# Value weights multiplied into the output weights inside a fused mLSTM and attention layer

## The chip, the cores and the metric

The kernel runs on one core of one Trainium2 chip. The metric is the device time of one execution in microseconds, the median over several runs; lower is better. A profiled execution stands beside the runs: it gives, for each instruction, the engine, the start and the duration.

The engines are TensorE (PE; its weight loads are PEld), VectorE (DVE), ScalarE (ACT), GpSimd (POOL) and SyncE (SP), which issues most transfers.

## The reference

One layer of a bidirectional encoder for 2048 tokens of width 1024, all in float32:

```python
h = rms_norm(x, g_mix_norm)
z = h @ w_in                       # 1024 -> 2000, split into nine parts
y_a = mlstm_group(q_m, k_m, v_m, o_m, gates, ...)          # (S, 512)
# group B: latent attention, 4 heads
q  = (rms_norm(c_q, g_cq) @ w_uq).reshape(B, S, 4, 192)
kv = (rms_norm(c_kv, g_ckv) @ w_ukv).reshape(B, S, 4, 256)
k_nope, v = kv[..., :128], kv[..., 128:]
# k gets a shared rotary part; q and k are normalised per head, rotary is applied
p = softmax(q_h @ k_h.T * 192 ** -0.5)
y_b = concat over heads of p @ v_h                          # (S, 512)
x = x + concat(y_a, y_b) @ w_out
h = rms_norm(x, g_ffn_norm)
x = x + square(relu(h @ w_ff1)) @ w_ff2
```

A fact of this algebra that the change uses: with `cn` the normalised latent of 128 numbers per token and `Wv_h` the 128x128 value part of `w_ukv` for head `h` (rows scaled by `g_ckv`), `v_h = cn @ Wv_h`. So `(p_h @ v_h) @ w_out[512 + 128 h :]` equals `(p_h @ cn) @ (Wv_h @ w_out[512 + 128 h :])`.

## The kernel before

Matmuls run as three products of a high and a low part (`mm3`): `split` casts a float32 tile to the high part on ACT and subtracts it on DVE (or on POOL where `eng` says so) for the low part.

The program has these stages. **First phase** (`phase_a`): tokens are normalised and transposed into `hh` and `hl`, eight tiles of 128 tokens at a time (two halves); all columns of `w_in` are projected. In each half there are eight `rest` tiles and then three blocks of eight tiles: `z_v`, `z_qk` (with a convolution on DVE, results in `ot`) and `z_o` (output gate). Each tile or channel group is 24 matmuls into one of two `pz` banks. `load_w` loads and splits the weights of a block; the split weights lie in pool `a_w`, the raw ones in `a_raw`.

Between those tiles `tick` places the work of latent attention (MLA), tile by tile, in four parts. `mla_a1` normalises the latent (`cn`, one buffer), transposes and splits it (`cTh`, `cTl`). `mla_a2` multiplies it with `wukh`, `wukl` (from `w_ukv`, keys and values of four heads interleaved, 1024 columns) and with the query weights into four `pm` banks, and forms squares on ACT. `mla_b1` copies the values out (`vn`, stored to `d_va`) and forms keys and queries on DVE. `mla_b2` transposes these and stores them to `d_kn`, `d_qn`, `d_kr`, `d_qr`. In this phase a scheduler orders the instructions by priority (program order, with `urgent` ahead) and by when they are expected to be ready.

**Attention** (`attention`): written out by hand, one step `g` for each score tile of 128 queries by 512 keys: five matmuls (`score`), the maximum on DVE, the exponential on ACT (`softmax`), four transposes and a split (`transpose_group`), and one `pv` step (three matmuls with `vh`, `vl`). `load_q`, `load_k`, `load_v` bring raw tiles into eight buffers of pool `stage`; `split_q`, `split_k`, `split_v` split them. Per head there are four K tiles and four V tiles. Two calls of `next(work)` per pair of steps bring in the mLSTM: first `mlstm_prelude` (gate tables, mostly small DVE operations), then `mlstm_steps`. Its loads `mlstm_v` and `mlstm_k` go through SP's queue.

**Output projection** (`OutProj`): `weights` loads and splits `w_out`; `load_b2` loads its lower half once more, for sums of weights. **Feed-forward** (`FeedForward`): two layers, each as seven products of halves.

SP's queue issues in order: a transfer that waits holds up all that stand behind it. Pools of attention lie over the pools of the first phase: `stage`, `k_sb` and `q_sb` on the right side of the memory, where the constants of latent attention (`wukh`, `wukl`, `wuqh`, ...) and its working tiles lay; `p_sb` over `hh`.

Of the kernel before, what the change touches and what calls it, by code (L numbers as in the profile page):

```python
# [8 lines left out]
F32 = mybir.dt.float32  # L9
# [79 lines left out]
def scratch(c, ctx):  # L89
# [9 lines left out]
    c.d_kr = dr.tile([NH, ROPE, S], F32, name="d_kr")  # L99
    c.d_va = dr.tile([S, 512], F32, name="d_va")  # L100
    c.d_ya = dr.tile([S, 512], F32, name="d_ya")
# [17 lines left out]
def phase_a(c):  # L119
    nc, tc = c.nc, c.tc  # L120
    with ExitStack() as st:
# [4 lines left out]
        hp = pool("a_h", 2)  # L126
        wp = pool("a_w", 9)
        rp = pool("a_raw", 5)
# [129 lines left out]
        def load_wu():  # L258
            for k in range(2):
                for j in range(2):  # L260
                    raw = rp.tile([P, 512], F32, name="raw")
                    cs = slice(j * 384, (j + 1) * 384)
                    nc.sync.dma_start(raw[:, :384], c.w_uq[k * P:(k + 1) * P, cs])
                    split(nc, wuqh[k][:, cs], wuql[k][:, cs], raw[:, :384], gcq[:, k:k + 1])
            for j in range(2):
                raw = rp.tile([P, 512], F32, name="raw")
                cs = slice(j * 512, (j + 1) * 512)
                nc.sync.dma_start(raw, c.w_ukv[:, cs])
                split(nc, wukh[:, cs], wukl[:, cs], raw, gcq[:, 2:3])

# [38 lines left out]
        def mla_a1(t, zr):  # L309
# [18 lines left out]
            with urgent():  # L328
                split(nc, ch, cl, pt[:, 0:3, :])
            mla_env[t] = [zr, ms3, ch, cl]  # L330

        def mla_a2(t):

            zr, ms3, ch, cl = mla_env[t]
            pk, pq = [], []
            for j in range(2):
                o = psM.tile([P, 512], F32, name="pm")
                cs = slice(j * 512, (j + 1) * 512)
                mm3(nc, o, ch[:, 2, :], cl[:, 2, :], wukh[:, cs], wukl[:, cs], True, True)
                pk.append(o)  # L340
            for j in range(2):
# [8 lines left out]
            qs = [pq[h // 2][:, (h % 2) * DH:(h % 2 + 1) * DH] for h in range(NH)]  # L350
            ks = [pk[h // 2][:, (h % 2) * 256:(h % 2) * 256 + NOPE] for h in range(NH)]
            for h in range(NH):
# [7 lines left out]
            rsqrt(c, r8, ms8, 8)  # L360
            mla_env[t] = [zr, pk, qs, ks, r8]

        def mla_b1(t):

            tok = slice(t * P, (t + 1) * P)
            zr, pk, qs, ks, r8 = mla_env[t]
            vn = mp.tile([P, NH, DV], F32, name="vn")
            for j in range(2):
                nc.scalar.copy(vn[:, 2 * j:2 * j + 2, :],
                               pk[j].rearrange("p (h d) -> p h d", h=2)[:, :, NOPE:])  # L370
            nc.sync.dma_start(c.d_va[tok, :], vn.rearrange("p h d -> p (h d)"))
            kpe = mp.tile([P, 1, ROPE], F32, name="kpe")
# [160 lines left out]
        for half in range(2):  # L533
# [27 lines left out]
            if half == 0:  # L561
# [5 lines left out]
                nc.sync.dma_start(c.d_r, rrow)  # L567
            nxt = []
            for blk in range(3):
                w = load_w((CV, CQ, CO)[blk], 512)  # L570
                if half == 0 and blk == 1:
                    load_r()
                for i in range(8):
                    n = blk * 8 + i
                    tick(n + 6 * half)
                    if half == 0 and blk == 2 and i >= 4:
                        prep_t(8 + i - 4, nxt)
                        if i == 7:
# [160 lines left out]
def mlstm_steps(c, pool, ps, ld):  # L739
# [185 lines left out]
    for n, grp in enumerate(groups):  # L925
        outs = [outer(kws.pop(ch), ld.pop(ch)[0]) for ch in grp]
        yield
        for k, ch in enumerate(grp):
            new = back[ch - 1] = advance(1, NT - 1 - ch, outs[k])
            if ch > 4:  # L930
                nc.sync.dma_start(c.d_C[ch - 1], new)
                ld[ch - 4] = mlstm_v(c, ch - 4), mlstm_k(c, ch - 4)
            if k == 0 and n + 1 < len(groups):
# [69 lines left out]
def attention(c, keep, drain, project):  # L1003

    nc, tc = c.nc, c.tc
    with ExitStack() as st:
# [41 lines left out]

        def load_v(h, j):
            raw = vraw[h, j] = rp.tile([P, 512], F32, name="raw").rearrange("p (k d) -> p k d", k=4)  # L1050
            nc.sync.dma_start(raw, c.d_va[j * 512:(j + 1) * 512, h * DV:(h + 1) * DV].rearrange(
                "(k p) d -> p k d", p=P))

        def split_v(h, j):
            raw = vraw.pop((h, j))
# [3 lines left out]
            V[h, j] = vh, vl  # L1059

# [80 lines left out]
        def pv(b, j, k):  # L1141
            h = b // NB
# [39 lines left out]
        load_v(0, 0)  # L1182
        load_v(0, 1)
        work = mlstm()
        def next_v(bp, j):
            h = bp // NB + 1
            if bp % NB == NB - 1 and h < NH:
                split_v(h, j)
                if j < 2:
                    load_v(h, j + 2)  # L1190

        for g0 in range(0, 16 * N, 2):
# [4 lines left out]
            for g in pair:  # L1197
                bp, n = divmod(g - 22, 16)
                if bp >= 0:
                    pv(bp, *divmod(n, 4))  # L1200
                    if n % 4 == 3:
                        next_v(bp, n // 4)
            if g0 % 16 == 4 and g0 > 32:
                out(g0 // 16 - 2)()
            for g in pair:
# [27 lines left out]
                if h < NH - 1:  # L1233
# [107 lines left out]
class OutProj:  # L1341
# [19 lines left out]
    def weights(self):  # L1361
# [985 lines left out]
```

## Time and profile before

| | us |
|---|---|
| median of 3 runs | 2545.44 (2545.09 to 2545.82) |
| profiled execution, time | 2542.08 |
| its span, first to last instruction | 2540.3 |
| PE busy | 2523.7 (99%) |
| PEld busy | 2111.3 (83%) |
| DVE busy | 1726.1 (68%) |
| ACT busy | 1293.7 (51%) |
| POOL busy | 380.7 (15%) |

The granted TensorE clock was 1.000 over the span. The first phase ends near 458 us, attention near 1130 us, the output projection and the first feed-forward layer near 1925 us. In the rows of the profile, `pm<-wukh,cTh` reads "output tile <- inputs" (the moving operand first, then the stationary one for matmuls); an `x` count follows, and times in brackets are idle time of the engine ahead of the row, with what ended it.

### The profile page before, as it was taken

The page shows a single profiled execution, that of the slowest core. Times are in us where ns is not written, and L with a number is a line of the kernel's source. Part 1 is how long each engine was busy: PE and PEld are TensorE (multiplying, and loading weights), DVE is VectorE, ACT ScalarE, POOL GpSimd, SP SyncE. Part 2 cuts the span into 40 slices and gives each one's busy share as a digit, 9 for nine tenths or more (in the row PEclk, how much of TensorE's full clock was granted, in tenths as well). Part 3 has the DMA queues.
Part 4 walks back from the last instruction along what each step waited for, and adds up shares of the span by engine and source line. Part 5 has one row for each costly group of instructions (what it writes and reads, how often), then busy time and mean ns, then how long its engine had stood idle before and what let it go on. Part 6 is the DMA issues. An engine that isn't in the chain of part 4 may idle for free. (4 is left out here: it accounts for less than half of the span.)

```text
span 2540.3 us, 35812 instructions
## 1 busy us (share of the span) xinstructions
PE 2523.7 (99%) x12380; PEld 2111.3 (83%) x12380; DVE 1726.1 (68%) x3286; ACT 1293.7 (51%) x2900; POOL 380.7 (15%) x428
## 2 busy tenths in 40 slices
PE   9999999999999999999999999999999999999999
PEld 7888888788888888888888888888888888888887
DVE  5585467766667667678788777977775577665433
ACT  6454444656767677674455555655554323332332
POOL 1211111223323332200000000000000232322000
PEclk9999999999999999999999999999999999999999
DMA  5434234355344343235786555654448544444552
GB/s 177 143 112 152 91 113 137 111 146 134 89 115 114 85 121 102 63 110 193 235 271 227 196 189 185 244 166 149 142 153 300 201 149 142 145 145 145 211 183 95
DMA packets 295931, 392.53 MB, mean 155 GB/s; under 512 B 32262, under 2 KB 176965, under 8 KB 295749
## 3 DMA queue, kind: packets, MB, share of 16 engines
q1 hardware_dynamic: 293284, 385.78, 48.0%
q10 hardware_dynamic: 2464, 4.46, 0.5%
q8 instruction: 97, 1.59, 0.3%
q14 instruction: 86, 0.70, 0.1%
HBM read 258.51 MB, written 131.64 MB: 154 GB/s over the span
## 5 line engine op out<-in xcount | busy, mean ns | idle before, releaser
L69 PE MATMUL pd<-w2h,uh 128*128 128x512 f32 x896 | 348.8, 389 | 0.1
L70 PE MATMUL pd<-w2l,uh 128*128 128x512 f32 x896 | 348.7, 389 | 0.0
L71 PE MATMUL pd<-w2h,ul 128*128 128x512 f32 x896 | 348.7, 389 | 0.0
L54 DVE TENSOR_TENSOR ul<-ur,uh 128x1024 fp32r<-128x1024 f32 x110 | 149.3, 1357 | 251.8 <-ACT uh L53 251.8
L53 ACT CAST uh<-ur 128x1024 fp32r<-128x1024 f32 x110 | 115.7, 1052 | 396.0 <-PE pd L70 382.4
L54 DVE TENSOR_TENSOR ptl<-ptp,pth 128x512 fp32r<-128x512 f32 x248 | 171.1, 691 | 190.0 <-ACT pth L53 188.9
L53 ACT CAST pth<-ptp 128x512 fp32r<-128x512 f32 x248 | 143.4, 578 | 157.7 <-PE ptp L1137 157.1
L2015 DVE TENSOR_TENSOR e<-pu,e 128x512 f32<-128x512 f32 x224 | 151.3, 689 | 88.7 <-PE pu L71 87.7
L69 PEld LDWEIGHTS pd<-w2h,uh 128*128 128x128 f32 x896 | 168.2, 188 | 35.4 <-DVE e L2015 0.5
L71 PEld LDWEIGHTS pd<-w2h,ul 128*128 128x128 f32 x896 | 168.2, 188 | 34.9
L70 PEld LDWEIGHTS pd<-w2l,uh 128*128 128x128 f32 x896 | 168.2, 188 | 34.8
L1106 ACT ACTIVATE p<-p,nm 128x512 f32<-128x512 f32 x256 | 185.8, 726 | 2.6 <-DVE nm L1099 2.6
L1095 DVE TENSOR_SCALAR_CACHE_REDUCE p<-ps 128x512 f32<-128x512 f32 x256 | 167.4, 682 | 15.2 <-PE ps L1094 15.1
L2179 POOL TENSOR_TENSOR r<-wr,r 128x512 f32<-128x512 f32 x48 | 81.5, 1697 | 621.1 <-DMA wr<-in_w 590.0
L69 PE MATMUL pz<-wh,hh 128*128 128x512 f32 (+1 forms) x384 | 149.5, 391 | 1.7 <-ACT vo L495 0.7
L71 PE MATMUL pz<-wh,hl 128*128 128x512 f32 (+1 forms) x384 | 150.0, 391 | 0.0
L70 PE MATMUL pz<-wl,hh 128*128 128x512 f32 (+1 forms) x384 | 149.2, 389 | 0.1
L2018 ACT ACTIVATE e<-e 128x512 f32<-128x512 f32 x128 | 80.9, 632 | 120.5 <-DVE e L2015 114.0
L1137 PE MATMUL ptp<-ident,p 128*128 128x128 f32 x992 | 130.6, 274 | 0.5 <-DVE ptl L54 0.3
L1137 PEld LDWEIGHTS ptp<-ident,p 128*128 128x128 f32 x992 | 113.6, 140 | 14.1 <-issue 1.4
L1090 PE MATMUL ps<-kh,qh 128*128 128x512 f32 x256 | 112.8, 441 | 2.4 <-DVE p L1095 2.4
L1883 ACT CAST r<-w1raw 128x512 fp32r<-128x512 f32 x104 | 64.6, 622 | 92.5 <-PE pu L71 92.5
(526 smaller groups left out, 6463.5 us busy)
## 6 DMA issues: line engine op xcount, KB each, us to landing
d_u<-e SPq DMA_DIRECT2D x224, 256.0 KB
ur<-d_u SPq DMA_DIRECT2D x110, 512.0 KB
wr<-in_w SPq DMA_DIRECT2D x96, 256.0 KB
w1raw<-in_w SPq DMA_DIRECT2D x42, 512.0 KB
raw<-in_w_in SPq DMA_DIRECT2D x48, 256.0 KB
r<-in_w SPq DMA_DIRECT2D x22, 512.0 KB
mb<-d_M SPq DMA_DIRECT2D x32, 256.0 KB
acc<-d_x SPq DMA_DIRECT2D x16, 512.0 KB
```

Of the source, the lines that this page charges most:

```text
L53: r = nc.scalar.copy(hi, src)
L54: (eng or nc.vector).tensor_tensor(lo, src, hi.bitcast(F32), op=ALU.subtract)
L69: nc.tensor.matmul(out, ah, bh, start=first, stop=False, skip_group_check=more)
L70: nc.tensor.matmul(out, ah, bl, start=False, stop=False, skip_group_check=more)
L71: nc.tensor.matmul(out, al, bh, start=False, stop=last, skip_group_check=more)
L1090: nc.tensor.matmul(o, qh[:, qs], kh, start=True, stop=False)
L1095: nc.vector.tensor_scalar(p, o, SCALE, None, op0=ALU.mult, op1=ALU.max, accum_out=maxes[b, a][:, j:j + 1])
L1106: nc.scalar.activation(p, p, AF.Exp, bias=maxes[b, a], accum_out=dens[b][:, a, j:j + 1])
L1137: nc.tensor.transpose(pt[:, k, :], p[:, k * P:(k + 1) * P], c.ident)
L2015: nc.vector.tensor_tensor(out, o, t, op=ALU.add)
L2018: nc.scalar.activation(t, t, AF.Relu)
L2179: nc.gpsimd.tensor_tensor(R, wr, R, op=ALU.subtract)
```

## The change

The value half of `w_ukv` is no longer multiplied with every token. It is scaled, transposed, split, and multiplied with the lower half of `w_out` once (`value_rows`), 8 products of 128x512, stored to `d_wv` on ACT's queue. Attention's `pv` multiplies the probabilities with `cn` (stored to `d_cn`), the same for all heads, so that it is loaded and split once. Both places that loaded the lower half of `w_out` load `d_wv`. Some loads and splits in attention change place or engine.

```diff
-    c.d_va = dr.tile([S, 512], F32, name="d_va")
+    c.d_cn = dr.tile([S, P], F32, name="d_cn")
+    c.d_wv = dr.tile([NH * P, D], F32, name="d_wv")
...
-        wp = pool("a_w", 9)
+        wp = pool("a_w", 10)
...
-            for j in range(2):
-                raw = rp.tile([P, 512], F32, name="raw")
-                cs = slice(j * 512, (j + 1) * 512)
-                nc.sync.dma_start(raw, c.w_ukv[:, cs])
-                split(nc, wukh[:, cs], wukl[:, cs], raw, gcq[:, 2:3])
+            raw = load_ukv(0)
+            split(nc, wukh[:, 0:512], wukl[:, 0:512], raw, gcq[:, 2:3])
+
+        def load_ukv(i):
+            raw = rp.tile([P, 512], F32, name="raw")
+            nc.sync.dma_start(raw.rearrange("p (h d) -> p h d", h=NH),
+                              c.w_ukv.rearrange("p (h t d) -> p h t d", h=NH, t=2)[:, :, i, :])
+            return raw
+
+        def value_rows():
+            raw = load_ukv(1)
+            nc.scalar.activation(raw, raw, AF.Copy, scale=gcq[:, 2:3])
+            yield
+            pt = psT.tile([P, 4, P], F32, name="pt")
+            for h in range(NH):
+                nc.tensor.transpose(pt[:, h, :], raw[:, h * P:(h + 1) * P], c.ident)
+            split(nc, wukh[:, 512:], wukl[:, 512:], pt.rearrange("p h d -> p (h d)"))
+            yield
+            pieces = {}
+
+            def load(n):
+                h, j = divmod(n, 2)
+                pieces[n] = rp.tile([P, 512], F32, name="raw")
+                nc.sync.dma_start(pieces[n], c.w_out[512 + h * P:512 + (h + 1) * P, j * 512:(j + 1) * 512])
+
+            def part(n):
+                wh = wp.tile([P, 512], F32R, name="wh")
+                wl = wp.tile([P, 512], F32R, name="wl")
+                split(nc, wh, wl, pieces.pop(n))
+                if n + 3 < 2 * NH:
+                    load(n + 3)
+                parts.append((wh, wl))
+
+            parts = []
+            for n in range(3):
+                load(n)
+            part(0)
+            yield
+            for n in range(2 * NH):
+                h, j = divmod(n, 2)
+                if n + 1 < 2 * NH:
+                    part(n + 1)
+                wh, wl = parts.pop(0)
+                o = psM.tile([P, 512], F32, name="pm")
+                hs = slice(512 + h * P, 512 + (h + 1) * P)
+                mm3(nc, o, wukh[:, hs], wukl[:, hs], wh, wl, True, True)
+                w = ep.tile([P, 520], F32, name="ot")[:, 0:512]
+                nc.scalar.copy(w, o)
+                nc.scalar.dma_start(c.d_wv[h * P:(h + 1) * P, j * 512:(j + 1) * 512], w)
+                if n < 6:
+                    yield
...
         def mla_a2(t):
-            zr, ms3, ch, cl = mla_env[t]
-            pk, pq = [], []
-            for j in range(2):
-                o = psM.tile([P, 512], F32, name="pm")
-                cs = slice(j * 512, (j + 1) * 512)
-                mm3(nc, o, ch[:, 2, :], cl[:, 2, :], wukh[:, cs], wukl[:, cs], True, True)
-                pk.append(o)
+            zr, ms3, ch, cl, cn = mla_env[t]
+            nc.sync.dma_start(c.d_cn[t * P:(t + 1) * P, :], cn[:, 256:384])
+            pq = []
+            pk = psM.tile([P, 512], F32, name="pm")
+            mm3(nc, pk, ch[:, 2, :], cl[:, 2, :], wukh[:, 0:512], wukl[:, 0:512], True, True)
...
         def mla_b1(t):
-            vn = mp.tile([P, NH, DV], F32, name="vn")
-            for j in range(2):
-                nc.scalar.copy(vn[:, 2 * j:2 * j + 2, :],
-                               pk[j].rearrange("p (h d) -> p h d", h=2)[:, :, NOPE:])
-            nc.sync.dma_start(c.d_va[tok, :], vn.rearrange("p h d -> p (h d)"))
...
+            rows = value_rows()
             for blk in range(3):
...
                     tick(n + 6 * half)
+                    if half and n >= 14:
+                        next(rows, None)
...  # mlstm_steps
         outs = [outer(kws.pop(ch), ld.pop(ch)[0]) for ch in grp]
+        for ch in grp:
+            if ch > 4:
+                ld[ch - 4] = mlstm_v(c, ch - 4), mlstm_k(c, ch - 4)
         yield
...
                 nc.sync.dma_start(c.d_C[ch - 1], new)
-                ld[ch - 4] = mlstm_v(c, ch - 4), mlstm_k(c, ch - 4)
...  # attention
-        def load_v(h, j):
-            raw = vraw[h, j] = rp.tile(...)
-            nc.sync.dma_start(raw, c.d_va[j * 512:(j + 1) * 512, h * DV:(h + 1) * DV].rearrange(...))
+        def load_v(j):
+            raw = vraw[j] = rp.tile(...)
+            nc.sync.dma_start(raw, c.d_cn[j * 512:(j + 1) * 512, :].rearrange("(k p) d -> p k d", p=P))
...
-            vh, vl = V[h, j]
+            vh, vl = V[j]
...
-            ld = {ch: (mlstm_v(c, ch), mlstm_k(c, ch)) for ch in range(NT - 1, NT - 5, -1)}
-            yield from mlstm_prelude(c, psM)
+            for n, _ in enumerate(mlstm_prelude(c, psM)):
+                if n == 10:
+                    ld = {ch: (mlstm_v(c, ch), mlstm_k(c, ch)) for ch in range(NT - 1, NT - 5, -1)}
+                yield
...
-                    split_k(h + 1, u - 3, nc.vector if u == 6 else nc.gpsimd)
-                    if u == 6:
-                        load_v(h + 1, 0)
-                        load_v(h + 1, 1)
+                    split_k(h + 1, u - 3, nc.gpsimd if u == 4 else nc.vector)
...
-                if g in (6, 8, 10, 12):
-                    split_v(0, g // 2 - 3)
-                    if g < 10:
-                        load_v(0, g // 2 - 1)
+                if g in (2, 4, 6, 8):
+                    load_v(g // 2 - 1)
+                if g in (16, 18, 20, 22):
+                    split_v(g // 2 - 8)
...  # OutProj.weights and OutProj.load_b2
-            nc.sync.dma_start(raw, c.w_out[k * P:(k + 1) * P, :])
+            nc.sync.dma_start(raw, c.d_wv[(k - 4) * P:(k - 3) * P, :])
...
-                                     self.c.w_out[(4 + k) * P:(5 + k) * P, half * 512:(half + 1) * 512])
+                                     self.c.d_wv[k * P:(k + 1) * P, half * 512:(half + 1) * 512])
```

The value splits of the later heads (`next_v`, called behind `pv`) and the two first loads of values ahead of the loop go as well. In `value_rows`, the call at `n` = 14 loads the value half, 15 transposes it, 16 loads the first pieces, 17 to 22 form one product each, 23 the last two, each ahead of that step's projection tile.

More of the change, by code (lines that the diff above doesn't have):

```diff
@@ L329, in mla_a1 @@
                 split(nc, ch, cl, pt[:, 0:3, :])
-            mla_env[t] = [zr, ms3, ch, cl]
+            mla_env[t] = [zr, ms3, ch, cl, cn]
         def mla_a2(t):
-            zr, ms3, ch, cl = mla_env[t]
-            pk, pq = [], []
-            for j in range(2):
-                o = psM.tile([P, 512], F32, name="pm")
-                cs = slice(j * 512, (j + 1) * 512)
-                mm3(nc, o, ch[:, 2, :], cl[:, 2, :], wukh[:, cs], wukl[:, cs], True, True)
-                pk.append(o)
+            zr, ms3, ch, cl, cn = mla_env[t]
[3 more added lines that the diff above has]
+            mm3(nc, pk, ch[:, 2, :], cl[:, 2, :], wukh[:, 0:512], wukl[:, 0:512], True, True)
             for j in range(2):
@@ L350, in mla_a2 @@
             qs = [pq[h // 2][:, (h % 2) * DH:(h % 2 + 1) * DH] for h in range(NH)]
-            ks = [pk[h // 2][:, (h % 2) * 256:(h % 2) * 256 + NOPE] for h in range(NH)]
+            ks = [pk[:, h * NOPE:(h + 1) * NOPE] for h in range(NH)]
             for h in range(NH):
@@ L360, in mla_a2 @@
             rsqrt(c, r8, ms8, 8)
-            mla_env[t] = [zr, pk, qs, ks, r8]
+            mla_env[t] = [zr, qs, ks, r8]
         def mla_b1(t):
-            tok = slice(t * P, (t + 1) * P)
-            zr, pk, qs, ks, r8 = mla_env[t]
-            vn = mp.tile([P, NH, DV], F32, name="vn")
-            for j in range(2):
-                nc.scalar.copy(vn[:, 2 * j:2 * j + 2, :],
-                               pk[j].rearrange("p (h d) -> p h d", h=2)[:, :, NOPE:])
-            nc.sync.dma_start(c.d_va[tok, :], vn.rearrange("p h d -> p (h d)"))
+            zr, qs, ks, r8 = mla_env[t]
             kpe = mp.tile([P, 1, ROPE], F32, name="kpe")
@@ L1047, in split_k, with split_v @@
             K[h, j] = kh, kl, rh, rl
-        def load_v(h, j):
[L1050 to L1055, printed above, removed]
+        def load_v(j):
+            raw = vraw[j] = rp.tile([P, 512], F32, name="raw").rearrange("p (k d) -> p k d", k=4)
+            nc.sync.dma_start(raw, c.d_cn[j * 512:(j + 1) * 512, :].rearrange("(k p) d -> p k d", p=P))
+        def split_v(j):
+            raw = vraw.pop(j)
             vh = vp.tile([P, 4, DV], F32R, name="vh")
@@ L1058, in split_v @@
             split(nc, vh, vl, raw, eng=nc.gpsimd)
-            V[h, j] = vh, vl
+            V[j] = vh, vl
         def load_q(h, j):
@@ L1141, in pv @@
         def pv(b, j, k):
-            h = b // NB
             if (j, k) == (0, 0):
@@ L1181, in attention @@
             split_k(0, j, nc.gpsimd if j == 2 else nc.vector)
-        load_v(0, 0)
-        load_v(0, 1)
         work = mlstm()
[L1185 to L1190, printed above, removed]
         for g0 in range(0, 16 * N, 2):
@@ L1200, in attention @@
                     pv(bp, *divmod(n, 4))
-                    if n % 4 == 3:
-                        next_v(bp, n // 4)
             if g0 % 16 == 4 and g0 > 32:
```

## Prediction

> **What bounds the kernel now.** I read the page first, then busy time by stage, then the start times of TensorE (PE) in order.
>
> ```profile
> PE 2523.7 (99%) x12380; PEld 2111.3 (83%) x12380; DVE 1726.1 (68%) x3286; ACT 1293.7 (51%) x2900; POOL 380.7 (15%) x428
> PE 35%; DVE 0%; issue 0%; ACT 0%; DVEq 0%
> 50.00:460.00 410.00, 407.42 (x2017) 345.12 (x2015) 266.36 (x695) 196.92 (x598) 64.76 (x102) 1.00 0.41 130
> 460.00:1130.00 670.00, 666.82 (x3843) 564.65 (x3842) 460.33 (x1184) 458.94 (x1268) 178.89 (x188) 1.00 0.41 107
> ```
>
> PE is busy in 407 of 410 us of the first phase and in 667 of 670 us of attention; no other engine passes 70% of either. The chain that ended last names PE lines only. But busy is not work: neighbouring matmuls overlap in the records. What a matmul costs is the step from its start to the next start.
>
> ```profile
> 437.76 0.39 PE L70 MATMUL pz<-wl,hh 128*128 128x512 f32 x1
> ...
> 444.79 0.39 PE L71 MATMUL pz<-wh,hl 128*128 128x512 f32 x1
> ...
> 448.64 0.60 PE L464 MATMUL pt<-ident,ot 128*128 128x128 f32 x4
> 449.08 0.27 PE L476 MATMUL pt<-ident,ot 128*2 128x128 f32 x1
> 449.11 0.47 PE L69 MATMUL pz<-wh,hh 128*128 128x512 f32 x1
> 449.42 0.39 PE L70 MATMUL pz<-wl,hh 128*128 128x512 f32 x1
> ...
> 457.74 0.39 PE L71 MATMUL pz<-wh,hl 128*128 128x512 f32 x1
> ```
>
> From 437.76 to 444.79 lie 31 steps: 0.2268 us each, although each record lasts 0.39. Four transposes take 0.44 us (448.64 to 449.08), and the first matmul behind transposes takes 0.31 instead of 0.23 (449.11 to 449.42), 0.09 more. I price every matmul by its step: the 0.39 of the groups would make the saving 1.7 times too large.
>
> **The change, part by part.** First the projection of values and its replacement.
>
> ```profile
> L69 PE MATMUL pm<-wukh,cTh x32: 390/396/505, 57.5 to 416.7; 128*128 128x512 f32 x32
> L71 PE MATMUL pm<-wukh,cTl x32: 387/393/477, 60.8 to 418.5; 128*128 128x512 f32 x32
> L70 PE MATMUL pm<-wukl,cTh x32: 390/393/399, 57.8 to 416.9; 128*128 128x512 f32 x32
> L369 ACT COPY vn<-pm x32: 351/365/401, 62.7 to 420.6; 128x256 f32<-128x256 f32 x32
> L53 ACT CAST vh<-raw x16: 603/618/620, 467.7 to 1004.4; 128x512 fp32r<-128x512 f32 x16
> L54 POOL TENSOR_TENSOR vl<-raw,vh x16: 1267/1280/1367, 468.4 to 1005.1; 128x512 fp32r<-128x512 f32 x16
> ```
>
> Of the 96 matmuls on `w_ukv` (three groups of 32) the value half goes: 48 x 0.2268 = 10.89 us off PE. Value products add 8 x 3 matmuls of the same shape, 5.44 us, and four transposes with the switch behind them, 0.53. Net on PE: -4.92 us. All of it lies in the first phase, where PE has no slack, so I count it in full. The number of matmuls in attention's `pv`, in the output projection and behind it stays; only what they multiply changes.
>
> ACT loses 32 copies (11.7 us by their 365 ns) and 12 `vh` casts (7.4); it gains one scaling, nine casts and eight copies, 18 x about 0.6 = 10.8, and issues eight stores. DVE gains nine subtractions of 0.69, less one of `w_ukv`: 5.5 us near 400 to 458. POOL loses 12 subtractions of 1.28. DMA swaps sixteen 256 KB stores for 64 KB ones and drops twelve 256 KB loads, against sixteen 256 KB transfers for weights. None of this enters the sum by itself: in attention ACT and DVE stand at 69%, in the first phase at 48% and 65%, and PE covers them. If that cover went, DVE's 5.5 us would be the price.
>
> One rule of the Trainium skill bears on the PE price: "TensorE: Matmul & The Clock Gate", section "Wait — 56ns, not 53.3ns?", has a warm step of N / 2.4 GHz plus about 2.5 ns, 215.8 ns at N = 512. The trace has 226.8 at a granted clock of 1.00. By the page the net would be -4.65 us; the measured step decides.
>
> **The hand-over to attention.** Here the change adds a wait. In the program before, stage buffers 5, 6 and 7, into which attention loads raw Q and K, lie at the bytes of `wukh` and `wukl`, the first loads take buffers 0, 7, 6, 5 in that order, and a buffer is written only when the last reader of every earlier tile under it is done. Before, those weights are last read at 418.5 (rows above). After, the last value product reads them, by program order just ahead of the last output-gate tile, at `i` = 7. SP's queue is in order, so every Q and K load but the first stands behind that product.
>
> ```profile
> 428.81 1.14 SPq L1067 DMA_DIRECT2D raw<-d_qr  x2
> 430.00 0.59 SPq L1033 DMA_DIRECT2D raw<-d_kn  x1
> ...
> 439.53 1.13 SPq L1036 DMA_DIRECT2D raw<-d_kr  x2
> 440.70 0.58 SPq L1033 DMA_DIRECT2D raw<-d_kn  x1
> ...
> 444.03 0.62 ACT L53 CAST rh<-raw 128x512 fp32r<-128x512 f32 x1 [2.54 <-DMA raw<-d_kr]
> 444.68 0.69 DVE L54 TENSOR_TENSOR rl<-raw,rh 128x512 fp32r<-128x512 f32 x1
> ...
> 453.37 0.75 DVE L455 SCALAR_TENSOR_TENSOR ot<-acc,cb,sg 128x514 f32<-128x514 f32 x1 [0.86 <-ACT sg L452]
> ```
>
> From the last value product: 1.14 + 0.59 us of issue, then the `d_kr` pair, 4.50 us from issue to its cast (439.53 to 444.03), 0.62 for the cast and 0.69 for the low part: 7.5 us. The first score needs that at its fifth matmul, 0.9 us after the last projection matmul: lead wanted 6.6 us. The lead there is one tile, 24 x 0.2268, plus transposes 0.47: 5.9. That is 0.7 us of stall, and each of the three further K tiles takes 1.7 us of issue while a score group uses 1.13: up to 1.7 more. Bounds: 0 when the value products run a tile earlier, 8.3 (6.6 + 1.7) when the last one runs behind the last tile. I take 1.7, from the place that program order gives it.
>
> **Three stalls that the edits touch.**
>
> ```profile
> 71.54 0.39 PE L71 MATMUL pz<-wh,hl 128*128 128x512 f32 x1
> 73.30 0.44 PE L325 MATMUL pt<-ident,cn 128*128 128x128 f32 x2 [1.37 <-DVE cn L321]
> ...
> 55.54 0.72 ACT L56 ACTIVATE wukh<-raw,vec 128x512 fp32r<-128x512 f32 x1 [1.65 <-DMA raw<-in_w_ukv]
> ...
> 70.07 1.13 DVE L383 SCALAR_TENSOR_TENSOR kn<-pm,r,gk 128x128 f32<-128x128 f32 x4 [1.57 <-POOL r L65]
> ...
> 471.25 0.50 PE L1090 MATMUL ps<-kh,qh 128*128 128x512 f32 x1 [0.69 <-DVE p L1095]
> ...
> 468.37 1.30 POOL L54 TENSOR_TENSOR vl<-raw,vh 128x512 fp32r<-128x512 f32 x1 [13.25 <-PE ps L1094]
> ...
> 468.62 1.20 DVE L649 TENSOR_TENSOR ln<-ln,d 128x128 f32<-128x128 f32 x1
> 469.86 0.29 DVE L650 SCALAR_TENSOR_TENSOR f<-f,ln 128x128 f32<-128x128 f32 x1
> ...
> 769.62 1.30 POOL L54 TENSOR_TENSOR rl<-raw,rh 128x512 fp32r<-128x512 f32 x1
> ...
> 769.66 2.53 DVE L890 TENSOR_TENSOR rd<-rd,gn 128x4 f32<-128x4 f32 x2
> ```
>
> At 71.5 PE waits 1.37 us for `cn`, which DVE writes behind `kn`, itself 1.57 late because ACT's squares were late. Two `vn` copies and the second `w_ukv` cast, 2 x 0.37 + 0.72 = 1.5 us, leave ACT ahead of those squares; ACT also waited for DMA there, so I take a third, -0.5, bounds 0 and -1.37.
>
> At 471 PE waits 0.69 us for DVE, which had been held at `ln`: 1.20 us for 128x128 while POOL subtracts a value tile, against 0.29 for the next one alone. The value splits move from `g` = 6..12 to 16..22, behind that part of the prelude: -0.7, bounds 0 and -0.7. The same holds where heads change: two 128x4 operations take 2.53 us beside POOL's split of K. One K split per head moves to DVE (two subtractions, 1.4 us more there, hidden at 69%), twelve value splits vanish: -0.4, bounds 0 and -0.8 (all these stalls are estimates from the rows of DVE).
>
> The four value splits at their new place could hold DVE in turn. The row says what is held: an operation with both inputs in SBUF. At 16..22 PE waits for `p<-ps` and `ptl<-ptp,pth`, which read PSUM and at most one SBUF tile, so I price it at nothing; 4 x 1.28 = 5.1 us is the bound if they were held too. "SBUF — State Buffer" of the Trainium skill, section "Who interferes with whom", states just this border: a DVE instruction with two SBUF inputs contends with a GpSimd one that reads SBUF, one with a single input outside the 2-port modes does not. By that rule the 5.1 falls away; the rows of `ln` agree.
>
> Loads moved inside attention (`mlstm_v`, `mlstm_k` earlier in the steps, later at the start) put a wait for `outer`'s matmul in front of SP's queue; the stores of `d_C` queue behind it for about a step, and nothing in PE's order waits for these within a group. Nothing for that. A tenth weight buffer lets the last weights be split one earlier; nothing for that either.
>
> **Sum** for the profiled execution (2542.08 us, span 2540.3): -4.92 + 1.7 - 0.5 - 0.7 - 0.4 = -4.8 us. It ran 3.4 us under the median shown (2545.44), so I apply the difference to the median: 2540.6 us. 0.2% of the time is 5.1 us, about what a measurement of this kernel can tell from no change: the forecast lies right at that edge.
>
> **Rivals.** First, the other side: the value products slip behind the last projection tile (`wh` has two spare buffers for them, `ot` is shared with the convolution's output, DVE has 5.5 us more). Then the hand-over costs 8.3 us, the sum is +1.8, 2547.2 us. It decides for slower by more than 0.2% once the last value product ends 3.3 us behind the last tile, since 6.5 us of gains plus 5.1 must be eaten: 2550.6 us or more. For it: DVE already runs behind here, its last convolution result comes at 453.4 to 454.1, only 4 us ahead of PE's last projection matmul. Against: each step has a whole tile (5.4 us) for 1.3 us of work.
>
> Second, `cn` has one buffer, and its next write now waits for the store to `d_cn`.
>
> ```profile
> L322 DVE TENSOR_SCALAR cn<-zr,r x16: 278/282/286, 18.9 to 411.2; 128x128 f32<-128x128 f32 x16
> 150.00:200.00 50.00, 50.00 (x246) 42.21 (x245) 43.67 (x118) 25.95 (x76) 8.02 (x11) 1.00 0.42 129
> ```
>
> A write comes every (411.2 - 18.9) / 15 = 26 us, a transfer lands in about 4.5, so SP must hold the store for over 20 us before DVE, and PE behind it, stands. It decides at 9.9 us (the 4.8 and 5.1), 0.7 on PE in each of 15 periods: 2550.5 us; with half of that, 2545.6.
>
> Third, the change takes work from PE and the time doesn't follow, because DVE is the bound: 43.67 of 50 us at 150 to 200. With the PE time of 2.5 latent tiles (0.68 each) gone, the stretch is 48.3 us and DVE at 90%: near, but not over. If it bound, only the stalls and the hand-over would remain: 2545.5 us.
>
> **How the numbers follow.** The case summed above: 0.68 (0.42 of it beyond 0.2%, as the stalls add up; 0.26 inside). Value products late: 0.15 (0.09 inside, 0.06 slower). `cn` held: 0.06 (0.02 inside, 0.04 slower). DVE as the bound: 0.07 (0.04 inside, 0.03 slower). The latent tiles, which now take three of four `pm` banks, run earlier and free more than I count: 0.04, faster. So faster 0.46, within 0.41, slower 0.13. Range: low from all stalls at their far bound and no hand-over, -4.92 - 1.37 - 0.7 - 0.8 = -7.8, with a little for the last case: 2536.5; high takes in the late value products: 2547.5.
>
> **What would show it.** Right: 48 matmuls fewer on `wukh` and `wukl` and 24 of the value products; the stretch from 50 us to the first score shorter by some 5 us; a PE gap of 1 to 3 us at the first scores with DMA `raw<-d_kn` as what ended it; no gap of 0.7 us while DVE works on `ln`. Wrong: a gap of 6 us or more there, `cn` waiting on DMA, weight casts of the last block waiting longer, or new PE waits for `ptl` while POOL splits values.

## The result, and the profile after

The changed kernel takes 2561.34 us (median of 4 runs, 2560.37 to 2563.54) against 2545.27 us for the program before on the same chip (2543.39 to 2545.82): ratio 1.0066, 95% interval 1.0048 to 1.0083. It is 16 us slower; the prediction was 2540.6 us, with a range of 2536.5 to 2547.5. The profiled execution took 2560.72 us with a span of 2558.8 us.

First the engines of the changed kernel, from its page, then busy time by stage (columns: the stretch, its length, busy time and instructions of PE, PEld, DVE, ACT, POOL, then the granted clock, the DMA share and GB/s):

```profile
PE 2525.4 (99%) x12360; PEld 2110.8 (82%) x12360; DVE 1726.8 (67%) x3300; ACT 1293.2 (51%) x2873; POOL 353.0 (14%) x410
50.00:450.00 400.00, 393.30 (x1941) 333.71 (x1940) 262.13 (x688) 189.88 (x560) 59.80 (x94) 1.00 0.38 121
450.00:500.00 50.00, 36.33 (x151) 26.89 (x150) 25.71 (x78) 29.46 (x60) 6.19 (x10) 0.86 0.68 199
500.00:1130.00 630.00, 628.46 (x3643) 533.36 (x3642) 428.95 (x1101) 421.83 (x1189) 154.55 (x168) 1.00 0.38 97
```

The same three stretches of the program before:

```profile
50.00:450.00 400.00, 397.42 (x1966) 337.20 (x1965) 260.92 (x686) 193.80 (x592) 63.63 (x96) 1.00 0.41 129
450.00:500.00 50.00, 47.89 (x240) 38.35 (x239) 37.74 (x106) 33.34 (x77) 11.50 (x14) 1.00 0.39 109
500.00:1130.00 630.00, 628.92 (x3655) 534.21 (x3654) 428.02 (x1088) 428.73 (x1198) 168.53 (x180) 1.00 0.41 108
```

The loss has a place. Attention behind 500 us is as busy as before (628.5 and 628.9 of 630 us). From 450 to 500 us PE works 36.3 us instead of 47.9, at a mean clock of 0.86, and it does 151 instructions instead of 240. A smaller loss lies ahead of 450 us (the next paragraph has its size).

To add such losses up I take, for every PE instruction, the step to the next start less the lower quartile of the steps of its shape, and sum; I call that lost time. It holds waits and slow steps alike. Before: 59.8 us in all (13.6 up to 450 us, 5.5 from 450 to 500, 32.2 in attention behind, 8.5 in the rest). After: 83.0 us (19.4, 20.5, 33.5, 9.7). By the same count the work itself shrank by 5.0 us (4.9 were forecast), so 23.2 - 5.0 = 18.2 us, and the spans differ by 18.5. All lost times here are of one profiled execution of each kernel.

PE in the changed kernel at the hand-over to attention, in order of time:

```profile
450.06 0.60 PE L281 MATMUL pt<-ident,raw 128*128 128x128 f32 x4
...
451.66 0.39 PE L71 MATMUL pz<-wh,hl 128*128 128x512 f32 x1
...
453.04 0.50 PE L69 MATMUL pm<-wh,wukh 128*128 128x512 f32 x1 [0.56 <-ACT wukh L53]
...
459.12 0.49 PE L69 MATMUL pm<-wh,wukh 128*128 128x512 f32 x1 [1.29 <-ACT ot L313]
...
460.81 0.51 PE L69 MATMUL pm<-wh,wukh 128*128 128x512 f32 x1 [0.73 <-ACT ot L313]
...
461.38 0.40 PE L71 MATMUL pm<-wh,wukl 128*128 128x512 f32 x1
470.47 0.80 PE L1133 MATMUL ps<-kh,qh 128*128 128x512 f32 x1 [8.69 <-ACT ot L313]
471.07 0.63 PE L1134 MATMUL ps<-kl,qh 128*128 128x512 f32 x1
471.49 0.63 PE L1135 MATMUL ps<-kh,ql 128*128 128x512 f32 x1
...
473.20 0.63 PE L1134 MATMUL ps<-kl,qh 128*128 128x512 f32 x1
```

The value half, called at tile 15 of the second half, is transposed only at 450.06, under the last projection tile, whose last matmul starts at 451.66 (457.74 before). All eight products run behind that tile, the last matmul from 461.38 on, with waits for their own copies; then PE stands 8.7 us. The first scores step by 0.427 us instead of 0.227. What ACT did meanwhile:

```profile
452.41 0.58 ACT L53 CAST wukh<-pt 128x512 fp32r<-128x512 f32 x1
...
460.17 0.59 ACT L313 COPY ot<-pm 128x512 f32<-128x512 f32 x1 [1.10 <-DMA d_wv<-ot]
...
462.46 0.58 ACT L313 COPY ot<-pm 128x512 f32<-128x512 f32 x1 [1.71 <-DMA d_wv<-ot]
...
466.88 0.58 ACT L313 COPY ot<-pm 128x512 f32<-128x512 f32 x1 [2.28 <-DMA d_wv<-ot]
467.36 0.62 ACT L1119 CAST qr<-raw 128x512 fp32r<-128x512 f32 x1
...
469.83 0.58 ACT L313 COPY ot<-pm 128x512 f32<-128x512 f32 x1 [1.33 <-DMA d_wv<-ot]
470.32 0.62 ACT L53 CAST rh<-raw 128x512 fp32r<-128x512 f32 x1
```

The copies wait for one of two `ot` buffers, which a store to `d_wv` holds until it has landed, and the casts of Q and K stand behind the copies in ACT's order. SP's queue, from the waits of 450 to 475 us (total, times, longest), was held as well: the Q load by the last value product, as the prediction said, the K loads by the stores:

```profile
SPq L1110 <- PE pm L71: 2.9, 1, 2.9
...
SPq L1077 <- DMA d_wv<-ot: 2.4, 2, 1.9
```

### The profile page after: what moved, and what is told of

Its sections match the earlier page's. It is cut to its first block, busy times and chain, and to the rows that moved or that the text cites. A ratio compares the mean times of both kernels' runs of the same rounds, so it can differ in the third digit from the quotient of the medians.

```text
span 2558.8 us, 35734 instructions
## 1 busy us (share of the span) xinstructions
PE 2525.4 (99%) x12360; PEld 2110.8 (82%) x12360; DVE 1726.8 (67%) x3300; ACT 1293.2 (51%) x2873; POOL 353.0 (14%) x410
```

## The experiments

Theory A: the products ran late, and the loads and casts of attention waited for them and their copies. Against it stood that only one of these waits matters (B), or that the time went in the first phase and in attention's edits (C). Each result below is against the program before, measured beside it on the same chip; one microsecond is 0.04%.

| kernel | median us | ratio, 95% interval | lost time on PE: up to 450, 450 to 500 us |
|---|---|---|---|
| changed kernel | 2561.3 | 1.0066, 1.0048 to 1.0083 | 19.4, 20.5 |
| own | 2558.9 | 1.0055, 1.0042 to 1.0067 | 19.0, 17.9 |
| psm | 2557.1 | 1.0049, 1.0037 to 1.0062 | 18.3, 16.2 |
| early | 2554.0 | 1.0037, 1.0025 to 1.0050 | 20.6, 15.4 |
| own_early | 2550.4 | 1.0026, 1.0015 to 1.0036 | 17.9, 14.9 |
| apart | 2549.3 | 1.0021, 1.0012 to 1.0030 | 18.4, 12.1 |
| no_rows | 2539.5 | 0.9983, 0.9974 to 0.9992 | 18.1, 7.4 |
| half0 | 2545.8 | 1.0005, 0.9996 to 1.0014 | 18.9, 8.3 |
| half0_xt3 | 2544.8 | 0.9999, 0.9990 to 1.0009 | 19.3, 3.5 |
| h0_psm | 2540.2 | 0.9980, 0.9971 to 0.9988 | 13.9, 4.3 |

**Own buffers for the copies (own).**

```diff
-                w = ep.tile([P, 520], F32, name="ot")[:, 0:512]
+                w = ep.tile([P, 512], F32, name="wv", bufs=4)
```

> The eight value copies get a tile of their own with four buffers instead of the two that they share with the convolution's output; nothing else changes, and all eight products still stand behind the last projection tile. Theory A (the time went into the hand-over: late products, and ScalarE held by copies that wait for a free buffer, with the casts of Q and K queued behind them): the copies no longer wait for their stores, the first score comes some 4 us earlier than 470.5 us and the time is about 2557 us. Rival B (only the stage loads that wait for the last product matter, the copies don't): no change, 2561. Rival C (the loss sits in the first phase and in attention's edits): no change, 2561.

2.4 us came back, between the 4 of theory A and the nothing of B, and the intervals of the two kernels overlap: this run alone doesn't decide. PE then waited 9.83 us for `kh`, and ACT for K's load (rows of PE and ACT, and SP's waits):

```profile
467.94 0.80 PE L1133 MATMUL ps<-kh,qh 128*128 128x512 f32 x1 [9.83 <-ACT kh L53]
467.27 0.62 ACT L53 CAST kh<-raw 128x512 fp32r<-128x512 f32 x1 [2.27 <-DMA raw<-d_kn]
SPq L1077 <- DMA d_wv<-wv: 3.3, 1, 3.3
```

So the copies' waits are at most the smaller part. Behind them stands the load, which still waits for the last products and, by SP's waits, for a store to `d_wv`. Which dependency ties a K load to that store the profile doesn't show.

**Earlier transposes (early), and both (own_early).**

```diff
-                    if half and n >= 14:
+                    if half and (n in (6, 7) or n >= 16):
```

> The value half is loaded and transposed at tiles 6 and 7 of the second half instead of 14 and 15; the copies still share the convolution's two buffers. In PE's order five of the eight products now stand ahead of the last projection tile, three behind it. Theory A: the last product still ends behind the last tile and its copies still wait, but fewer of them; the gap ahead of the first score falls from 8.9 us to 4 to 6 us, time about 2556 us. Rival B: the last product ends about 3 us earlier relative to the last tile, time about 2558. Rival C: 2561.

> Both edits at once: own buffers for the copies and the value half transposed at tiles 6 and 7. In PE's order the last two products stand one tile ahead of the end. Theory A: the gap ahead of the first score falls from 8.9 us to 0 to 2 us, the stalls behind it go as well, and of the 14.9 us that the stretch from 450 to 500 us lost most comes back: about 2548 us, within 5 us of the program before. Rival B: about the same gap, since the loads are released early, but no further gain: 2553. Rival C: 2558 to 2561, still slower than before by 0.5%.

Early transposes bring about 7 us, both edits 10 to 11. In own_early the first score waits 1.82 us for `kh` instead of 8.7. C falls: moving these few operations took away two thirds of the loss. Against theory A's 2548 some 2 us are missing: PE still loses 15 us from 450 to 500, in slow steps and a gap of 3 us at 466 us.

**The bank of the transposes (psm).** Why did they run some 50 us (nine tiles) behind their call? In PE's order they stood behind the transposes of a convolution, which uses the same two `pt` banks.

```diff
-            pt = psT.tile([P, 4, P], F32, name="pt")
+            pt = psM.tile([P, 512], F32, name="pm").rearrange("p (k t) -> p k t", k=4)
```

> One line differs from the changed kernel: the four transposes of the value half write into a bank of the group pm instead of the group pt, whose two banks they shared with the convolution's transposes. In PE's order they then stand at tile 58.9 instead of 63.75, and five of the eight products stand ahead of the last projection tile instead of none. Theory A (the products were late because their transposes stood in line for a pt bank behind a convolution that runs some 50 us behind PE): about as the run with early transposes, 2554 us. Rival F (the products are late by their weights, whose buffers come free only while the last tile runs): no change, 2561.

With this one line the transposes run at 418.90 instead of 450.06 (a row of PE, then the group of products with first and last start):

```profile
418.90 0.60 PE L281 MATMUL pm<-ident,raw 128*128 128x128 f32 x4
L69 PE MATMUL pm<-wh,wukh x8: 387/454/481, 425.8 to 456.5; 128*128 128x512 f32 x8
```

Rival F (late by their weights) falls for the first products, which now start at 425.8, not 453.0. The last one still runs at 457.0, behind the last projection tile (454.8), and the time falls by 4 us only, with overlapping intervals. In early it was the same (458.4), and own buffers in place of the shared `ot` pair brought it forward to 449.1 (own_early). So the `pt` banks held the first products, the `ot` pair the last.

What decides is the last product: its last matmul starts 8.1 to 10.2 us ahead of the first score in all five kernels so far (9.1 in the changed kernel, 10.2 in own, 8.1 in early, 8.9 in psm, 8.3 in own_early), wherever it stands.

**Value weights not under attention's stage (apart).** As own_early, with `wvh` and `wvl` on the other side of the memory (the products read these; three buffers for the copies instead of four; shown is the main part of the edit).

```diff
-            split(nc, wukh[:, 512:], wukl[:, 512:], pt.rearrange("p h d -> p (h d)"))
+            wvh = gp.tile([P, 512], F32R, name="wvh")
+            wvl = gp.tile([P, 512], F32R, name="wvl")
+            split(nc, wvh, wvl, pt.rearrange("p h d -> p (h d)"))
```

> As the kernel with own buffers (three here) and the early transposes, with one thing more: the value weights get two tiles of their own on the left side of the memory, so that no stage buffer lies over what the value products read. PE's order is the same. Theory A1 (the reuse of wukh's and wukl's bytes holds Q's and K's loads until the last value product): the loads go out some 15 us earlier, the 2 us gap ahead of the first score, the 3 us gap at 466 us and the half-clock steps between them vanish; about 2543 us against 2550.4. Rival A2 (what is left is work in ScalarE's and VectorE's queues at the hand-over): no change, 2550.

A1's mechanism is there, its price isn't: the loads go out from 425 us on, and the first score stands right behind the last projection tile (455.48 after 455.25), 5.7 us behind the last product. But the time falls by 1 us, inside the intervals. Other waits ended last instead (waits of PE from 440 to 480 us):

```profile
PE pt L517 <- ACT kt L519: 2.8, 1, 2.8
PE ps L1135 <- ACT wv L315: 1.5, 1, 1.5
```

**No products at all (no_rows).** `value_rows` isn't called.

> The value products are left out altogether, and the two places that load them load the lower half of the output weights as they are (so the result lacks the multiplication with the value weights); everything else of the change stays. Theory A: 14.9 us of stalls and 6 us of PE work go, and what is left is the pure saving of 48 matmuls, 10.9 us, less the stalls that the first phase gained elsewhere (about 6 us by its windows): about 2540 us. Rival C: the loss stays, 2552 us or more.

This splits the 16 us. Against before, the changed kernel has +16.1 and no_rows -4.8; of the 20.9 between them 6.0 are PE's work, so 14.9 us are stalls of the products. And of the 10.9 us that 48 matmuls are worth, 6.1 do not arrive. Lost time points at two places, in rows of PE and ACT of this kernel:

```profile
242.54 0.47 PE L69 MATMUL pz<-wh,hh 128*128 128x464 f32 x1 [0.68 <-ACT hh L53]
244.48 1.11 PE L164 MATMUL pt<-ident,xt 128*128 128x128 f32 x4 [1.25 <-DVE hl L54]
453.24 0.26 ACT L517 COPY kt<-pt 2x128 f32<-2x128 f32 x1 [3.95 <-DMA d_k<-kt]
453.40 0.72 ACT L491 ACTIVATE sg<-acc,vec 128x514 f32<-128x514 f32 x1
454.96 0.66 PE L503 MATMUL pt<-ident,ot 128*128 128x128 f32 x4 [1.74 <-DVE ot L494]
```

At the switch of halves (200 to 250 us: 4.3 us lost, 0.8 before) PE arrives earlier and finds the tokens not prepared. At the end (7.4 against 5.5) it finds the convolution not done: its sigmoid stands on ACT behind a copy of two rows that waits 3.95 us for a store. Three more runs without products took these chains away one at a time.

```diff
-        xp = pool("a_x", 2, "right")
+        xp = pool("a_x", 3, "right")
```

> Value products left out as in the run without them (the result lacks the multiplication with the value weights), and a third buffer for the rows of x that are prepared for the second half. At 242 us PE then waited 2.3 us for that preparation, ahead of which ScalarE waited for the transfer of x. Theory E (PE gains time in the first half, reaches the switch of halves earlier and finds the tokens not prepared, because a row tile of x loads only when one of two buffers is free): the gaps at 242 us go, 2537 us against 2539.5. Otherwise no change, and the gap at 242 stays.

2538.06 us, 0.9974 (0.9964 to 0.9984). Theory E holds in the profile: PE has no wait left between 230 and 260 us. In the time the 2 us are inside the intervals.

> Value products left out and three x buffers (as in the run before; the result lacks the multiplication with the value weights), and a second buffer each for the convolution's acc and sg, which are one each. Theory G (of the 10.9 us saved on PE some 3 are lost at the end of the first phase, because the convolution is a chain of its own that ends at 454 us whatever PE does, each of its tiles waiting for the one before to leave acc and sg): the 1.9 us gap ahead of the transposes of ot goes, and the time falls by 2 to 4 us to about 2535. Rival: the chain is bound by VectorE's own work or its order; no change, 2538.

2539.96 us, 0.9980 (0.9971 to 0.9988): no gain. (`acc` and `sg` got `bufs=2`.) The gap ahead of `ot`'s transposes is gone, as theory G says, but PE's order changed with it, and PE waits elsewhere instead, with half-clock steps behind:

```profile
454.77 0.48 PE L670 MATMUL pm<-ident,G 128*64 128x128 f32 x1 [3.59 <-ACT vo L534]
```

So theory G's gain in time falls; what the two buffers alone are worth stays open.

> Value products left out and three x buffers (2538.1 us; the result lacks the multiplication with the value weights), and a second buffer for the convolution's transposed output kt. Theory H (the end of the first phase is held by kt: ScalarE's copy of two rows waits up to 5 us for the store of the one kt buffer, and the sigmoids and the output gate's last tile wait behind it in ScalarE's queue): the gap of 1.9 us ahead of ot's transposes and the half-clock steps behind it go, and the time falls by 2 to 4 us to about 2535. Rival: the chain is held by the transfers' own queue, no change, 2538.

2530.66 us, 0.9941 (0.9929 to 0.9953), with one PE wait of 0.6 us (for `ptl`) left from 440 to 480 us: 14.5 us under the program before, more than the 10.9 of the matmuls. (`kt` got `bufs=2`.) But PE's order had changed with it (the last latent tile stands one projection tile earlier), and the pairs below show no gain from `kt`, so theory H isn't settled by this.

**The products in the first half (half0, half0_own).**

```diff
-                    if half and n >= 14:
+                    if half == 0 and n >= 14:
```

> Only the place changes: the value rows are formed at tiles 14 to 23 of the first half instead of the second, with everything shared as in the changed kernel. By PE's order the last product then stands at tile 31.8 of 64, behind it lies the second half. Theory A: the hand-over is as without the products, and PE's 6 us of product work remain: 2539.5 + 6 = about 2545.5 us, up to 3 us more if the products collide with the preparation of the second half. Rival D (products cost 20 us wherever they stand, by the load on ScalarE, VectorE and the weight buffers): 2555 us or more.

> As the run before, with four own buffers for the value copies. Theory A: in the first half no cast of attention stands behind the copies, so the shared pair costs little there: within 2 us of the run before, about 2544.5 us. If the ring still cost as it did in the changed kernel, 3 us or more would come back.

Here theory A's number came out: 2545.75 us, as no_rows plus 6 us. The same operations cost 15 us less 200 us earlier, and rival D falls. Own buffers bring nothing there (half0_own: 2548.1, 1.0012, 1.0003 to 1.0021), as theory A said for a place with no casts of attention behind the copies.

**Putting it together.** All with the products in the first half and three x buffers; `best` with two buffers for `acc` and `sg`, `h0_kt2` with two `kt`, `h0_psm` with the transposes in a bank of `pm`, `h0_psm_kt2` with both of the last.

> The run before without the second buffers for acc and sg: value rows in the first half and three x buffers. By the sum of the single effects 2545.75 - 1.4 = 2544.3 us. If the x buffers are worth more here, because the products stand right at the switch of halves where x is loaded, 2542.

> A version that might beat both: value rows in the first half, three x buffers, two buffers each for acc and sg. By the runs so far: 2545.75 for the first half alone, less 1.4 for the x buffers, less 3 if theory G holds: about 2541 us, 0.15% under the program before; without G 2544.

> The value rows in the first half with three x buffers (2544.8 us), and two kt buffers. Theory H: 2 to 4 us less, about 2542 us. Rival: 2545.

> As the run before, and the transposes of the value half write into a bank of the group pm; in PE's order the products then stand spread from tile 29.1 to 31.5 instead of in a lump up to 31.9 at the switch of halves. The gaps at 240 to 253 us, about 3 us in all in the run without this, should shrink: about 2540.5 us if theory H holds too, 2543 if not.

> The version that beat the program before (2540.1 us: value rows in the first half, their transposes in a bank of pm, three x buffers, two kt buffers) with one kt buffer again. In PE's order the products stand as spread as there (tiles 29.1 to 31.75). If the second kt buffer carried the gain (theory H), 2543 to 2545 us, as in the run with three x buffers alone (2544.8); if the spread of the products carried it, 2540.

half0_xt3 2544.8; best 2544.45 (0.9999, 0.9990 to 1.0008); h0_kt2 2546.47 (1.0002, 0.9993 to 1.0011); h0_psm_kt2 2540.14 (0.9978, 0.9969 to 0.9988); h0_psm 2540.19 (0.9980, 0.9971 to 0.9988). The bank makes the difference in both pairs, by 4.6 and 6.3 us, and a second `kt` buffer none in two of three pairs. (Of the three only h0_psm and h0_psm_kt2 have the latent tiles at the same place of PE's order; in h0_kt2 the last one stands a projection tile later than in half0_xt3.) PE's waits of half0_xt3 from 230 to 260 us, and the hand-over of h0_psm, which has no wait at all between 230 and 260:

```profile
PE pz L69 <- ACT zr L339: 2.1, 1, 2.1
PE pz L70 <- DVE wl L57: 1.0, 1, 1.0
PE pz L69 <- ACT wh L56: 0.8, 1, 0.8
450.00:500.00 50.00, 48.91 (x249) 39.41 (x249) 36.76 (x112) 36.05 (x84) 12.66 (x16) 1.00 0.30 85
```

With `pt`, five of the eight products stand in the last tile ahead of the switch of halves, where ACT and DVE prepare x and weights (half0_xt3); with `pm` three do, and the first starts at tile 29.1 instead of 30.0 (h0_psm). That the spread, and not the bank by itself, removes the waits is argued from these rows, not tested apart. h0_psm is the version that beats both kernels: 5.1 us under before, 21 under the changed kernel.

> The version that beat the program before, with the value rows begun at tile 11 of the first half's blocks instead of 14: in PE's order the products stand at tiles 24.1 to 28.3, three tiles clear of the switch of halves, where x and the next weights are loaded. Without products the same buffers gave 2530.7 us, and the products are 6 us of work on PE: 2536.7 if nothing else is lost. If the place of the products no longer matters once they are spread, 2540.

Too early loses the gain: 2547.04 us (1.0007, 0.9998 to 1.0016). In ACT's order a cast of the value pieces now comes ahead of the casts of the next block's weights, which wait for their loads, and PE waits for that block (lost time from 150 to 200 us: 9.5, against 0.8 in h0_psm):

```profile
192.59 0.73 PE L69 MATMUL pz<-wh,hh 128*128 128x512 f32 x2 [2.74 <-ACT wh L56]
```

**Control.**

> A control: the program before with three x buffers and two kt buffers and nothing of the change. There PE is later at both places (the switch of halves and the end of the first phase) than in the changed kernels, so the buffers should be worth nothing: 2544.9 us, within 1.5.

2544.07 us, 0.9993 (0.9985 to 1.0002): the buffers are worth nothing measurable without the change. So h0_psm owes its gain to the change, once its place and bank are mended; half0_xt3, with the place alone, only draws level.

## Why the prediction was wrong, step by step

**The work on PE, -4.92: right as work, wrong as time.** The count fits: PE has 20 instructions fewer (24 matmuls less, four transposes more). The step that failed is "PE has no slack, so I count it in full". Busy near 100% says that PE never stood for long at its present pace; it doesn't say that the others could keep up with a faster one. Without any product 4.8 of 10.9 us arrived. In the changed kernel the lost time ahead of 450 us grew by 5.8, more than the net saving. That the term can arrive h0_psm shows: 5.1 us less than before, with lost time as before (59.2 us in all).

**The stall at 71.5, -0.5: wrong sign, and the clearest example.** PE, DVE and PE again:

```profile
70.70 0.39 PE L71 MATMUL pz<-wh,hl 128*128 128x512 f32 x1
73.48 0.44 PE L372 MATMUL pt<-ident,cn 128*128 128x128 f32 x2 [2.39 <-DVE cn L368]
...
74.91 0.63 PE L70 MATMUL pz<-wl,hh 128*128 128x512 f32 x1
75.33 0.63 PE L71 MATMUL pz<-wh,hl 128*128 128x512 f32 x1
...
73.08 0.35 DVE L368 TENSOR_SCALAR cn<-zr,r 128x256 f32<-128x256 f32 x1
```

PE arrives 0.84 us earlier than before, three matmuls of a latent tile and their share of the lead; the second part of `cn` still starts at 73.34 (73.16 before). The lost time of the gap grew by 1.0 us, from 1.53 to 2.55, instead of shrinking, and half-clock steps followed.

**The hand-over, +1.7 within 0 to 8.3: this step failed most.** "I take 1.7, from the place that program order gives it" was the error: the products' place was set by buffers that they shared with the convolution (the `pt` banks, then the `ot` pair), not by the call. My sentence "each step has a whole tile (5.4 us) for 1.3 us of work" priced the steps as if each could begin when called. Rival 1 had the case, with 0.15 and 2547.2 us; its condition (the last product more than 3.3 us behind the last tile) held with 461.4 against 451.7, and the sign I had named, a gap of 6 us or more, came with 8.7. Its price was little more than half of what came: 8.3 against 14.9 us. The load path alone, from the last product to the first score, took 9.1 us where I had 7.5 to the fifth matmul. Three things were not in my bound: the products' own waits (0.7 + 1.5 + 0.9 us of lost time), the gaps of 0.7 and 2.0 us behind the first scores, and slow steps (13 with 0.2 us each by 484 us). `ot` shared with the convolution I had named only as a cause of lateness, not as a hold on ACT's queue.

**The stalls at `ln` and at the change of head, -0.7 and -0.4.** Where the hand-over is calm the first is gone (h0_psm loses 4.3 us from 450 to 500, before 5.5). In attention behind 500 us lost time moves between 31.5 and 33.5 over these kernels, 32.2 before: -0.4 can't be told from nothing.

**The other rivals.** `cn` held by its store: no; PE waits for `cn` once, at 71 us. DVE as the bound: not by its busy share, 67%, but the idea was near. What PE runs into is a chain of other engines at three places: `cn` at 71 us, the preparation of x at 242, the convolution's last tiles at 453. The tenth weight buffer wasn't tried alone. `ptl` against POOL's value splits at their new place costs nothing to be seen: PE's waits for `ptl` are 0.9 us in all in the changed kernel.

## What to carry to other kernels

A saving on a saturated engine arrives only where nothing else is due at that moment: before counting it, move the engine forward in the trace by the saving and ask, at each of its waits, when the other engine's result comes. New work that borrows from a ring, a set of buffers used in turn (here banks that matmuls write to, and output buffers), runs at the time of the chain that it shares the ring with, not where it is called: look where the chain stands in the trace, not in the code. Put one-off work where nothing on an in-order queue stands behind it, in a bank that no late chain holds, and look in the new trace at what it now stands ahead of.

## What the hardware showed that I had not expected

PE fell to half pace after short waits: steps of 0.427 us against 0.227, for 2.6 to 3.1 us, after 8.7 us of idling at 461 us, after only 2.39 at 70.7 (rows above), and, from 480.7 us on, after waits of 0.56 and 1.67. The length of the wait alone doesn't decide: with gaps between 2.3 and 2.7 us of lost time at the place of 70.7, 6 of 15 kernels of this case slowed down and 9 didn't. In h0_psm 2.28 us of idling had no such effect:

```profile
74.27 0.44 PE L372 MATMUL pt<-ident,cn 128*128 128x128 f32 x2 [2.28 <-DVE cn L368]
...
75.46 0.39 PE L70 MATMUL pz<-wl,hh 128*128 128x512 f32 x1
75.69 0.40 PE L71 MATMUL pz<-wh,hl 128*128 128x512 f32 x1
```

The granted clock in the traces tells more. Half clock comes there in stretches of 3.41 us or whole multiples (but for the last one, cut off by the end), and where a trace has several, they start on one grid of 3.41 us. I laid that grid over the 20 traces: from full clock, every window of it in which PE stood for more than 2.0 us was followed by half clock, none with less than 1.5 us was, and in between both occur. At the place of 70.7 us the six kernels have 1.87 to 2.39 us of their idling inside one window, the nine at most 1.79. So there it is the border of the window that makes the difference.

A slow spell costs about 1.4 us here, so a wait can cost half as much again as it lasts. The Trainium skill, "TensorE: Matmul & The Clock Gate", section "What's actually happening", has PE at half clock after at least one idle window of about 3.4 us of a free-running counter, and its section "Wait — 56ns, not 53.3ns?" has a half-clock step of N / 1.2 GHz, 426.7 ns at N = 512. The step agrees with the 0.427 us here and the window with the 3.41; that half clock can come after 2.39 us of idling, with no window idle throughout, doesn't agree, and the measurement decides.
